# First blocks of x by halves, both differential copies on ScalarE, gate products ahead of weight splits, last router logits ahead of the rank sums

## The chip, the cores and the metric

One Trainium2 chip, one core. The metric is the device time of one launch in microseconds (us); a time given for a kernel is the median of several launches. A launch of the kernel before takes 967.19 us (three runs, 966.83 to 968.14).

Engines: TensorE (PE, matmul and transposes; PEld are its weight loads), VectorE (DVE), ScalarE (ACT), GpSimd (POOL) and SyncE (SP), whose queue issues nearly all DMA here. Each engine works through its own instructions in program order and waits for the others through semaphores.

## What is computed

The reference is one decoder layer on x (512 tokens x 1024, float32), followed by a last RMSNorm:

```python
h = rms_norm(x, g_mix)
fq, fk, fv, f_logit, dq, dk, dv, gate_a, gate_b = split(h @ w_in)
y_a = fox_attention(fq, fk, fv, cumsum(log_sigmoid(f_logit + b)))      # 8 heads of 64, causal
y_b = diff_attention(rope(dq), rope(dk), dv, lam)                       # 4 heads: p1 - lam * p2, causal
y_b = rms_norm(y_b, g_diff_sub) * (1 - lambda_init)
x = x + (sigmoid(gate_a) * (y_a @ w_branch_a) + sigmoid(gate_b) * (y_b @ w_branch_b)) @ w_out
x = x + cross_attention(rms_norm(x, g_cross), rms_norm(mem, g_mem))     # 4 heads, 256 memory tokens
x = x + moe(rms_norm(x, g_ffn))      # top 1 of 4 groups, then top 2 of its 8 SwiGLU experts
return rms_norm(x, g_final)
```

The weights of the 32 experts are 1024 x 512 (gate, up) and 512 x 1024 (down), all float32.

## The kernel before

**Products in two parts.** Every large product is made from operands that are split into a rounded high part and the low rest: `split` (L175 to L177) is a ScalarE copy into the high part (L176) and a VectorE subtraction into the low part (L177). A product then takes three matmuls for each block of 128 of the contraction: high times high, and the two mixed ones (L278 to L280 in the profile). Activations are split into HH and HL (`hh`, `hl` in the profile), weights into `wh` and `wl`.

**Weights of the mixer** come through a stream object `W` in halves of 512 KB: `load` issues the DMA on SP into a raw buffer `wr`, `split` makes `wh` and `wl` of a half, and `W.more()` splits the next half that is due. `W.lazy` says that a unit doesn't call it by itself.

**The first stage** (L318 to L360): x comes in transposed, one block `xT` of 128 x 1024 for each of the four token tiles t. `h_gain` multiplies it by the gain of the norm (VectorE, L326), `h_split` makes hh and hl from it, in two halves of 512 columns each. `nat_unit` (L301) then makes the product with the first 256 columns of the Fox values for tile t: 24 matmuls of 128 x 256 into a bank `fv0p`, and returns its copy out of the bank (L306), which scales by the tile's inverse norm `rT`. The norm itself is taken from the untransposed x: `h_stat(t)` calls `rms_stat` (L251), one ScalarE Square with a sum over 1024 columns, Ln, Exp, and four small VectorE instructions, for each tile. Behind the four units stand the 16 matmuls of the forget logits `pz` (L365, L366), four small ones that spread rT over the partitions (`pR`, L370), and the next unit, `fq0`.

**The attention steps** (L925 to L987): one loop over 16 Fox steps and then 8 Diff steps (two head pairs g, four query tiles b). A Diff step issues in this order: scores (`sd`, L543, with the mask matmuls L673), the softmax (L683 to L685), one unit of other work (a gate unit `w..p` or a branch unit `br`, 24 or 12 matmuls of 128 x 512), the product with the values of the step before, `combine` (VectorE), `W.more()`, the end of the unit's work `ev()`, a second unit, `W.more()` again, the transposes `trans` (`td`, L275), `copy` (L708 to L713) and the second unit's `ev()`. `copy` moves the two transposed banks `td` to `pd` so that the next step's products can read them: the first on VectorE, the second on ScalarE, both recorded at L711. The next step's scores are written to the same four banks, so that they wait for these copies. The end of a gate unit is a VectorE product (L829) and a ScalarE tanh (L830), that of a branch unit a VectorE instruction (L846).

**The routing** (L1315 to L1318): the work behind the output projection follows a table that is written out by hand, one letter for each function. `R` makes the router logits of a token tile (`lg`, 8 matmuls and a ScalarE copy, L1146), `L` transposes them back (`lgt`, L1153, and VectorE L1154), `z` is one step of the ranking of experts (14 small steps for each tile, of which the last writes the mask `Mb`, L1213), `r` sums the mask over the tokens before (`pr`, L1231) and makes the rank `rk` (L1233), `o` makes the one-hot matrix `G` of the first four experts (L1238), `g` gathers tokens with it (`ga`, 4 matmuls for each entry, L1244), and `H` splits the normalised x (`hnh` on ScalarE, L1129; `hnl` on VectorE, L1130).

**The experts** follow: their weights, 4 MB and 2 MB for each expert, stream through a ring of 1 MB pages whose loads are issued on SP (L1269), each as soon as the work on the page's old content is done. `gu` are the gate and up products (L1479).

Order on every engine is that of the code; the framework puts the semaphore waits, and nothing is reordered afterwards.

Of the kernel before, what the change touches and what calls it, by code (L numbers as in the profile page):

```python
# [10 lines left out]
F32 = mybir.dt.float32  # L11
F32R = mybir.dt.float32r
BF = mybir.dt.bfloat16
# [5 lines left out]
P = 128  # L19
# [21 lines left out]
def tile_hybrid_block(  # L41
# [30 lines left out]
    def tiny(shape, name, dt=F32):  # L72
        return work(shape, dt, name, "tiny")
# [11 lines left out]
    def xt(t):  # L85
        return X[t // 2][:, t % 2]
# [20 lines left out]
    def xT(t, k0=0, n=KD):  # L107
        return XT[t // 2][:, t % 2, k0:k0 + n]
# [206 lines left out]
        gemm(o, KD, lambda k: wh[:, k, sl], lambda k: wl[:, k, sl], lambda k: hk(HH, k), lambda k: hk(HL, k))  # L315
        return lambda: evac(j, o)

    def h_split(t, qs=(0, 1)):  # L318

        sl = slice(t * P, (t + 1) * P)  # L320
        for q in qs:
            split(HH[q][:, :, sl], HL[q][:, :, sl], xT(t, 4 * q, 4))

    def h_gain(t, k0=0, n=KD):
        v = xT(t, k0, n)
        V.tensor_tensor(v, v, gm[:, k0:k0 + n, None].to_broadcast([P, n, P]), op=OP.mult)  # L326

    def h_stat(t):
        rms_stat(xt(t), f"nx{t}", out=rT[:, t:t + 1])


    warm = bank("warm", "a")
# [3 lines left out]
    W.lazy = True  # L336
    lg = c1.tile([P, KD, 16], F32R, name="lg")
    h_gain(0, 0, 4)
    h_split(0, (0,))
    W.split(1)  # L340
    h_gain(0, 4, 4)
    h_split(0, (1,))
    W.split(2)
    evs = []
    for t in range(NT):
        evs.append(nat_unit(c_fv[0], t, fv, 0, "fv0", tag="as"[t // 2]))
        if t + 1 < NT:
            h_gain(t + 1)
            h_split(t + 1)
        if t == 1:  # L350
            split(lg[:, :, 0:8], lg[:, :, 8:16], lg_r)
            W.split(3)
        if t == 2:
            h_stat(0)
            h_stat(1)
            evs.pop(0)()
            evs.pop(0)()
            h_stat(2)
            h_stat(3)
    W.lazy = False  # L360


# [296 lines left out]
    class Diff:  # L659
# [47 lines left out]
        def copy(self):  # L707
            self.pt = []  # L708
            for i in range(2):
                r = half([P, S], F32, f"pd{self.g}{self.b}{i}")  # L710
                (V.tensor_copy if i == 0 else A.copy)(r[:, 0:self.n], self.tb[i][:, 0:self.n])  # L711
                self.pt.append(r)

        def av(self):
# [212 lines left out]
    for n, it in enumerate(its):  # L927
        it.scores()
        it.soft()
        while late:  # L930
            late.pop(0)()
        fe = rows() if rows is not None else None
        ev = unit()
        if fe is not None:
            fe()
        fin2 = prev.av() if prev is not None else None
        if n == 1:
            swap_matrix()
        if n == 2:
            rotary_angles()  # L940
        if n == 3:
            rotary_tables()
        if n == 4:
            lam_calc()
        if n == 7:
            dv = page([P, NT, 512], F32, "dv")
        it.combine()
        if fin is not None and isinstance(done, Diff):
            done.scale()
        W.more()  # L950
        if isinstance(it, Diff):
            ev()
            while late:
                late.pop(0)()
            ev = unit()
            W.more()
        it.trans()
        if isinstance(it, Diff):
            it.copy()
            ev()  # L960
        else:
            ev()
            it.copy()
        if n == 5:
            rotary_spread()
        rows = fin
        if isinstance(it, Fox) and it.b == NT - 1 and it.pr < 3:
            Fox(it.pr + 1, 0).prep()
        if n == 15:
            YB["h"] = page([P, 4, S], F32R, "ybh")  # L970
            YB["l"] = page([P, 4, S], F32R, "ybl")
        done, prev, fin = prev, it, fin2
# [342 lines left out]
    for step in """T0 N0 U20 Q0 U21 K0 T1 N1 U30 U22 W Q1 S0 M0 K1 U23 U31 N2 T2 S1 P0 Q2 M1 U32 A0 U33 K2 T3 O0 N3 S2  # L1315
        M2 Q3 P1 X0 K3 F0 A1 S3 M3 P2 R0 O1 L0 P3 F1 z0.0 A2 X1 z0.1 z0.2 z0.3 z0.4
        z0.5 A3 z0.6 z0.7 z0.8 O2 z0.9 z0.10 z0.11 E E E E R1 z0.12 z0.13 H0 X2 F2 L1 r0 O3 o0 z1.0 z1.1 H1 z1.2 z1.3
        F3 z1.4 z1.5 R2 z1.6 z1.7 z1.8 X3 g0.0 z1.9 z1.10 L2 z1.11 z1.12 z1.13 H2 g0.1 z2.0 z2.1 r1 z2.2 R3 o1 z2.3  # L1318
        z2.4 g0.2 z2.5 z2.6 z2.7 L3 z2.8 g0.3 z2.9 z3.0 z2.10 z3.1 g1.0 z2.11 z3.2 z2.12 z3.3 z2.13 H3 g1.1 z3.4 r2
        z3.5 z3.6 o2 z3.7 g1.2 z3.8 z3.9 g1.3 z3.10 z3.11 g2.0 g2.1 z3.12 z3.13 g2.2 g2.3 r3 o3""".split():  # L1320
        f, t = step[0], int(step[1]) if len(step) > 1 else 0
        if f == "U":
            out_unit(t, int(step[2]))
        elif f == "E":
            EX.load(page)
        elif f == "W":
            W.split(2 * c_co + 2)
        elif f == "z":
            route_step(t)
        elif f == "g":  # L1330
            gather0(t, int(step[3]))
        elif f == "M":
            cross_soft(t)
            cross_scale(t)
        else:
            {"N": lambda t: x_stat(t, "nc"), "F": ffn_stat, "r": ranks, "o": lambda t: onehot(0, t), "X": x_trans, "T": cross_trans, "Q": cross_q, "K": cross_qt, "S": cross_scores, "P": cross_ptrans,
             "A": cross_av, "O": cross_out, "H": ffn_split, "R": router,
             "L": router_t}[f](t)
# [510 lines left out]
```

## Time and profile before

| | before |
|---|---|
| median of 3 launches | 967.19 us (966.83 to 968.14) |
| the profiled launch | 968.59 us |
| its span, first to last instruction | 966.8 us |
| mean granted TensorE clock | 0.994 of full speed |
| busy: TensorE, VectorE, ScalarE, GpSimd | 97%, 50%, 33%, 7% |
| read from memory | 243.65 MB |

How to read the rows. A row of the timeline gives the start in us from the span's beginning, the busy time in us, the engine, the line, the operation, output and inputs by their names in the program, the tile's shape, and the count (x2: two such instructions run together). Brackets at the end give the idle time of the engine ahead of the row and what ended it. A row of the view of waits gives the total, the number of times and the longest. A row of the table of windows gives, for a stretch of the span, its length, then the busy time of TensorE, its weight loads, VectorE, ScalarE and GpSimd with the number of instructions in parentheses, then the granted clock, the DMA engines' busy share, and GB/s. The share of busy DMA engines over the span in 40 slices, in tenths, shows where the experts' stream runs (from slice 23 on):

```profile
PE   7999999999999999999999999999999999999995
DMA  8221112221132228335669989999999999999993
```

### The profile page before, as it was taken

What the parts mean: (1) busy time and instruction counts of PE and PEld (TensorE: products, weight loads), DVE (VectorE), ACT (ScalarE), POOL (GpSimd) and SP (SyncE); (2) the same over time, 40 slices, a digit from 0 to 9 for tenths busy, and PEclk for the clock granted to TensorE, in tenths of its full rate; (3) what the DMA queues carried; (4) which work ended last, traced back from release to release, by engine and by line L of the source; (5) the groups of instructions that cost most, each with busy time, mean ns of one, the idle gap of its engine ahead of it and who ended that gap; (6) DMA issues with size and microseconds to landing.
All of it is one profiled execution on the core that took longest, in us unless ns stands there. A gap on an engine that the chain in (4) does not pass through costs nothing. (4 is left out here: it accounts for less than half of the span.)

```text
span 966.8 us, 13460 instructions
## 1 busy us (share of the span) xinstructions
PE 936.9 (97%) x5234; PEld 610.6 (63%) x5235; DVE 484.7 (50%) x1075; ACT 314.3 (33%) x675; POOL 64.5 (7%) x171
## 2 busy tenths in 40 slices
PE   7999999999999999999999999999999999999995
PEld 7787788787887889999743734343633436334332
DVE  6556775857665657655754333443323541243334
ACT  4444444545352445345521211111311112111114
POOL 1840000001111200000100000000000000000000
PEclk9999999999999999999999999999999999999998
DMA  8221112221132228335669989999999999999993
GB/s 320 85 70 66 58 53 66 66 87 44 66 131 87 87 87 283 128 136 233 247 243 411 389 335 420 421 420 422 420 421 421 422 421 420 422 420 421 421 414 119
DMA packets 48290, 246.65 MB, mean 255 GB/s; under 512 B 4832, under 2 KB 12256, under 8 KB 24160
## 3 DMA queue, kind: packets, MB, share of 16 engines
q1 hardware_dynamic: 48080, 245.76, 63.9%
q8 instruction: 42, 0.69, 0.3%
q14 instruction: 24, 0.20, 0.1%
q10 hardware_dynamic: 144, 0.00, 0.0%
HBM read 243.65 MB, written 2.10 MB: 254 GB/s over the span
## 5 line engine op out<-in xcount | busy, mean ns | idle before, releaser
L1479 PE MATMUL gu<-gu,xg 128*64 128x512 f32 x1024 | 223.9, 593 | 1.9 <-DMA gu<-in_w_gu_dram 1.8
L1479 PEld LDWEIGHTS gu<-gu,xg 128*64 128x64 f32 x1024 | 72.7, 137 | 146.4 <-issue 139.1
L1501 PE MATMUL yd<-dn,A 128*64 128x512 f32 x504 | 113.6, 596 | 0.0
L177 DVE TENSOR_TENSOR wl<-wr,wh 128x1024 fp32r<-128x1024 f32 (+1 forms) x66 | 78.1, 1191 | 31.9 <-ACT wh L176 31.2
L1523 DVE TENSOR_TENSOR xr<-cb,xr 128x512 f32<-128x512 f32 x120 | 74.5, 683 | 37.8 <-PE cb L1519 37.7
L1484 DVE SCALAR_TENSOR_TENSOR A<-A,gu 128x256 f32<-128x256 f32 x32 | 13.5, 421 | 157.7 <-ACT A L1483 157.7
L1501 PEld LDWEIGHTS yd<-dn,A 128*64 128x64 f32 x504 | 35.7, 137 | 67.4 <-issue 66.6
L1483 ACT ACTIVATE A<-gu 128x256 f32<-128x256 f32 x32 | 12.3, 383 | 202.2 <-PE gu L1479 202.2
L176 ACT ACTIVATE wh<-wr 128x1024 fp32r<-128x1024 f32 (+1 forms) x66 | 67.0, 1026 | 8.7 <-DVE wr L143 7.7
L1509 DVE SCALAR_TENSOR_TENSOR Y<-yd,ws,Y 128x512 fp32r<-128x512 f32 x32 | 23.9, 751 | 90.4 <-ACT Y L1508 85.6
L1519 PE MATMUL cb<-Y,ohT 128*128 128x512 f32 x240 | 65.0, 410 | 1.6 <-DVE xr L1523 0.5
L1508 ACT ACTIVATE Y<-yd,ws 128x512 fp32r<-128x512 f32 x32 | 21.9, 687 | 119.7 <-PE yd L1501 112.4
L1519 PEld LDWEIGHTS cb<-Y,ohT 128*128 128x128 f32 x240 | 42.9, 188 | 15.4 <-DVE xr L1523 4.3
L278 PE MATMUL wop<-wh,mh 128*128 128x256 f32 x128 | 36.7, 286 | 0.2 <-DVE xr L1023 0.2
L279 PE MATMUL wop<-wl,mh 128*128 128x256 f32 x128 | 36.2, 283 | 0.0
L280 PE MATMUL wop<-wh,ml 128*128 128x256 f32 x128 | 36.2, 283 | 0.0
L1446 PE MATMUL ga<-Gr,hnh 128*128 128x384 f32 x96 | 32.4, 337 | 0.0
L1446 PE MATMUL ga<-Gr,hnl 128*128 128x384 f32 x96 | 32.1, 334 | 0.0
L584 ACT ACTIVATE S<-S,bi 128x128 f32<-128x128 f32 (+3 forms) x32 | 17.8, 556 | 29.7 <-DVE bi L581 29.7
L278 PEld LDWEIGHTS wop<-wh,mh 128*128 128x128 f32 x128 | 24.5, 192 | 0.6 <-DVE xr L1023 0.4
L279 PEld LDWEIGHTS wop<-wl,mh 128*128 128x128 f32 x128 | 24.6, 192 | 0.0
L280 PEld LDWEIGHTS wop<-wh,ml 128*128 128x128 f32 x128 | 24.5, 192 | 0.0
(617 smaller groups left out, 1859.3 us busy)
## 6 DMA issues: line engine op xcount, KB each, us to landing
gu<-in_w_gu_dram SPq DMA_DIRECT2D x128, 1024.0 KB, 19.0
dn<-in_w_dn_dram SPq DMA_DIRECT2D x59, 1024.0 KB, 19.8
wr<-in_w_inp_dram SPq DMA_DIRECT2D x40, 512.0 KB, 3.6
wr<-in_w_out_dram SPq DMA_DIRECT2D x8, 512.0 KB, 5.8
dn<-in_w_dn_dram SPq DMA_DIRECT2D x6, 512.0 KB, 14.4
x<-in_x_dram SPq DMA_DIRECT2D x2, 1024.0 KB, 11.2
wr<-in_w_branch_a_dram SPq DMA_DIRECT2D x4, 512.0 KB, 3.6
wr<-in_w_branch_b_dram SPq DMA_DIRECT2D x4, 512.0 KB, 3.5
```

The costliest lines, as they stand in the source:

```text
L176: A.activation(hi, src, AF.Copy)
L177: V.tensor_tensor(lo, src, hi.bitcast(F32), op=OP.subtract)
L278: PE.matmul(o, lh, rh, start=first, stop=False)
L279: PE.matmul(o, lh, rl, start=False, stop=False)
L280: PE.matmul(o, ll, rh, start=False, stop=last)
L1446: PE.matmul(o, CX[u, t // 2][:, t % 2, kb * P:(kb + 1) * P], CX["G", r][:, t], start=(t == 0 and u == "h"), stop=(t == NT - 1 and u == "l"))
L1479: PE.matmul(gu[64 * f:64 * f + 64, :], xg(2 * i + j), w[:, :, j, 256 * f:256 * f + 256], start=(i + j == 0), stop=(i + j == 4))
L1501: PE.matmul(y[j][64 * a:64 * a + 64, :], hT[a][:, f % 2, f // 2], w(a, f)[:, j, f % 2], start=(f == 0), stop=(f == 3))
L1508: A.activation(yh[rows, j], y[j][rows], AF.Copy, scale=ws)
L1509: V.scalar_tensor_tensor(yl[rows, j], y[j][rows], ws, yh[rows, j].bitcast(F32), op0=OP.mult, op1=OP.subtract)
L1519: PE.matmul(banks[j], oh[:, t * P:(t + 1) * P], y[u][:, j], start=(u == 0), stop=(u == 1))
L1523: V.tensor_tensor(xs, banks[j], xs, op=OP.add)
```

## The change

It edits four places and leaves the arithmetic as it was, apart from the way in which one norm is summed.

1. First stage. The gain product of tiles 1 to 3 is made in two halves of 512 columns, each followed by its high part; the two low parts come behind both. The norms of the four tiles are made by one chain: three Squares on ScalarE and one multiply-and-sum on VectorE for the last tile, then one Ln, one Exp and five VectorE instructions of four columns instead of four chains of one column. The chain stands behind all parts of all tiles. The split of the forget weights `lg` and of the third weight half moves from behind tile 1 to behind tile 2. All four copies out of `fv0p` come behind the matmuls of `pR`; before, two stood ahead.
2. Diff steps. Both copies of `td` to `pd` are on ScalarE.
3. Diff steps. The end of the first unit's work (the gate product, or the branch product) stands ahead of the first `W.more()`.
4. Routing table. `R3` stands ahead of `r1`, the steps of tiles 2 and 3 are interleaved otherwise, and `H3` stands behind the last step of tile 3 instead of ahead of `g1.1`.

```diff
--- before.py
+++ after.py
@@ -315,18 +315,34 @@
         gemm(o, KD, lambda k: wh[:, k, sl], lambda k: wl[:, k, sl], lambda k: hk(HH, k), lambda k: hk(HL, k))
         return lambda: evac(j, o)
 
-    def h_split(t, qs=(0, 1)):
-
+    def h_hi(t, q):
+
+        A.activation(HH[q][:, :, t * P:(t + 1) * P], xT(t, 4 * q, 4), AF.Copy)
+
+    def h_lo(t, q):
         sl = slice(t * P, (t + 1) * P)
-        for q in qs:
-            split(HH[q][:, :, sl], HL[q][:, :, sl], xT(t, 4 * q, 4))
+        V.tensor_tensor(HL[q][:, :, sl], xT(t, 4 * q, 4), HH[q][:, :, sl].bitcast(F32), op=OP.subtract)
 
     def h_gain(t, k0=0, n=KD):
         v = xT(t, k0, n)
         V.tensor_tensor(v, v, gm[:, k0:k0 + n, None].to_broadcast([P, n, P]), op=OP.mult)
 
-    def h_stat(t):
-        rms_stat(xt(t), f"nx{t}", out=rT[:, t:t + 1])
+    def h_stat():
+
+        ss, ln, r0, v, w = (tiny([P, NT], f"nx_{n}") for n in "slrvw")
+        for t in range(NT):
+            junk = work([P, D], BF, f"nx{t}_j")
+            if t < NT - 1:
+                A.activation(junk, xt(t), AF.Square, accum_out=ss[:, t:t + 1])
+            else:
+                V.tensor_tensor_reduce(junk, xt(t), xt(t), 1.0, 0.0, OP.mult, OP.add, ss[:, t:t + 1])
+        A.activation(ln, ss, AF.Ln, scale=1.0 / D, bias=epsd)
+        A.activation(r0, ln, AF.Exp, scale=-0.5)
+        V.tensor_scalar(v, ss, 1.0 / D, 1e-6, op0=OP.mult, op1=OP.add)
+        V.tensor_tensor(w, r0, v, op=OP.mult)
+        V.tensor_tensor(w, w, r0, op=OP.mult)
+        V.tensor_scalar(w, w, -0.5, 1.5, op0=OP.mult, op1=OP.add)
+        V.tensor_tensor(rT, r0, w, op=OP.mult)
 
 
     warm = bank("warm", "a")
@@ -336,27 +352,27 @@
     W.lazy = True
     lg = c1.tile([P, KD, 16], F32R, name="lg")
     h_gain(0, 0, 4)
-    h_split(0, (0,))
+    h_hi(0, 0)
+    h_lo(0, 0)
     W.split(1)
     h_gain(0, 4, 4)
-    h_split(0, (1,))
+    h_hi(0, 1)
+    h_lo(0, 1)
     W.split(2)
     evs = []
     for t in range(NT):
         evs.append(nat_unit(c_fv[0], t, fv, 0, "fv0", tag="as"[t // 2]))
         if t + 1 < NT:
-            h_gain(t + 1)
-            h_split(t + 1)
-        if t == 1:
+            h_gain(t + 1, 0, 4)
+            h_hi(t + 1, 0)
+            h_gain(t + 1, 4, 4)
+            h_hi(t + 1, 1)
+            h_lo(t + 1, 0)
+            h_lo(t + 1, 1)
+        if t == NT - 2:
             split(lg[:, :, 0:8], lg[:, :, 8:16], lg_r)
             W.split(3)
-        if t == 2:
-            h_stat(0)
-            h_stat(1)
-            evs.pop(0)()
-            evs.pop(0)()
-            h_stat(2)
-            h_stat(3)
+            h_stat()
     W.lazy = False
 
 
@@ -708,7 +724,7 @@
             self.pt = []
             for i in range(2):
                 r = half([P, S], F32, f"pd{self.g}{self.b}{i}")
-                (V.tensor_copy if i == 0 else A.copy)(r[:, 0:self.n], self.tb[i][:, 0:self.n])
+                A.copy(r[:, 0:self.n], self.tb[i][:, 0:self.n])
                 self.pt.append(r)
 
         def av(self):
@@ -947,13 +963,13 @@
         it.combine()
         if fin is not None and isinstance(done, Diff):
             done.scale()
-        W.more()
         if isinstance(it, Diff):
             ev()
+            W.more()
             while late:
                 late.pop(0)()
             ev = unit()
-            W.more()
+        W.more()
         it.trans()
         if isinstance(it, Diff):
             it.copy()
@@ -1315,9 +1331,9 @@
     for step in """T0 N0 U20 Q0 U21 K0 T1 N1 U30 U22 W Q1 S0 M0 K1 U23 U31 N2 T2 S1 P0 Q2 M1 U32 A0 U33 K2 T3 O0 N3 S2
         M2 Q3 P1 X0 K3 F0 A1 S3 M3 P2 R0 O1 L0 P3 F1 z0.0 A2 X1 z0.1 z0.2 z0.3 z0.4
         z0.5 A3 z0.6 z0.7 z0.8 O2 z0.9 z0.10 z0.11 E E E E R1 z0.12 z0.13 H0 X2 F2 L1 r0 O3 o0 z1.0 z1.1 H1 z1.2 z1.3
-        F3 z1.4 z1.5 R2 z1.6 z1.7 z1.8 X3 g0.0 z1.9 z1.10 L2 z1.11 z1.12 z1.13 H2 g0.1 z2.0 z2.1 r1 z2.2 R3 o1 z2.3
-        z2.4 g0.2 z2.5 z2.6 z2.7 L3 z2.8 g0.3 z2.9 z3.0 z2.10 z3.1 g1.0 z2.11 z3.2 z2.12 z3.3 z2.13 H3 g1.1 z3.4 r2
-        z3.5 z3.6 o2 z3.7 g1.2 z3.8 z3.9 g1.3 z3.10 z3.11 g2.0 g2.1 z3.12 z3.13 g2.2 g2.3 r3 o3""".split():
+        F3 z1.4 z1.5 R2 z1.6 z1.7 z1.8 X3 g0.0 z1.9 z1.10 L2 z1.11 z1.12 z1.13 H2 g0.1 z2.0 z2.1 R3 z2.2 r1 z2.3 o1
+        z2.4 g0.2 z2.5 z2.6 L3 z2.7 g0.3 z2.8 z3.0 z2.9 z3.1 g1.0 z2.10 z3.2 z2.11 z3.3 z2.12 z3.4 g1.1 z2.13 z3.5
+        z3.6 r2 z3.7 z3.8 o2 g1.2 z3.9 g1.3 z3.10 z3.11 g2.0 g2.1 z3.12 z3.13 H3 g2.2 g2.3 r3 o3""".split():
         f, t = step[0], int(step[1]) if len(step) > 1 else 0
         if f == "U":
             out_unit(t, int(step[2]))
```

Lines behind the first stage have numbers higher by 16 in the changed kernel.

What this does to the order, at the three places that the prediction speaks of. VectorE, the first stage, from tile 2 on, before (`xT` the block and its gain, `hl` the low parts, `wl` the low part of a weight half, `nx_` the norm):

```order
L326 TENSOR_TENSOR xT_84<-xT_84,gm 128x1024
L177 TENSOR_TENSOR hl_115<-xT_84,hh_113 128x4x128
L177 TENSOR_TENSOR hl_116<-xT_84,hh_114 128x4x128
L177 TENSOR_TENSOR lg<-sma,lg 128x8x8
L177 TENSOR_TENSOR wl_217<-wr_94,wh_216 128x1024
L326 TENSOR_TENSOR xT_84<-xT_84,gm 128x1024
L177 TENSOR_TENSOR hl_115<-xT_84,hh_113 128x4x128
L177 TENSOR_TENSOR hl_116<-xT_84,hh_114 128x4x128
L263 TENSOR_SCALAR nx_v<-nx_ss 128x1
```

The same place in the changed kernel:

```order
L328 TENSOR_TENSOR xT_84<-xT_84,gm 128x512 x2
L324 TENSOR_TENSOR hl_115<-xT_84,hh_113 128x4x128
L324 TENSOR_TENSOR hl_116<-xT_84,hh_114 128x4x128
L328 TENSOR_TENSOR xT_84<-xT_84,gm 128x512 x2
L324 TENSOR_TENSOR hl_115<-xT_84,hh_113 128x4x128
L324 TENSOR_TENSOR hl_116<-xT_84,hh_114 128x4x128
L177 TENSOR_TENSOR lg<-sma,lg 128x8x8
L177 TENSOR_TENSOR wl_250<-wr_94,wh_249 128x1024
L338 ISA nx_j,nx_s<-x_76 128x1024
```

The gain products come in halves, and the parts of tile 3 now stand ahead of `lg` and `wl`. The last row is the VectorE sum of squares.

VectorE, the last Diff step of the loop, before (`zn` the normalised output of an earlier step, `g` the branch product):

```order
L736 TENSOR_TENSOR zn_3100<-zo_2805,rq_z 128x512
L177 TENSOR_TENSOR wl_3103<-wr_2853,wh_3102 128x1024
L846 SCALAR_TENSOR_TENSOR g_2779<-g_2779,br_3072 128x512
L711 COPY pd_3132<-td_3122 128x512
L846 SCALAR_TENSOR_TENSOR g_2779<-g_2779,br_3109 128x512
L177 TENSOR_TENSOR wl_3103<-wr_2982,wh_3102 128x1024
```

And in the changed kernel:

```order
L752 TENSOR_TENSOR zn_3071<-zo_2776,rq_z 128x512
L862 SCALAR_TENSOR_TENSOR g_2750<-g_2750,br_3043 128x512
L177 TENSOR_TENSOR wl_3075<-wr_2824,wh_3074 128x1024
L862 SCALAR_TENSOR_TENSOR g_2750<-g_2750,br_3080 128x512
L177 TENSOR_TENSOR wl_3075<-wr_2955,wh_3074 128x1024
```

The branch product has changed places with `wl`, and the copy of `td` is gone from VectorE; it stands on ScalarE, directly ahead of the other.

VectorE, the routing, from the mask of tile 2 on, before (`R` the ranking steps of tile 3):

```order
L1213 TENSOR_TENSOR Mb<-Wh_3886,Wh_3887 128x32
L1130 SCALAR_TENSOR_TENSOR hnl_5075<-xr_3759,nf_z,hnh_5074 128x1024
L1188 ISA R_5119,mm__3888<-L,R_5119 128x32
L1188 ISA mm__3888 128x1
L1233 TENSOR_TENSOR rk<-pr,Mb 128x32
L1191 SCALAR_TENSOR_TENSOR R_5119<-R_5119,mm__3888,down_3872 128x32
L1194 TENSOR_REDUCE R_5119<-R_5119 128x1
L1238 TENSOR_TENSOR G<-rk,slot_f 128x256
```

And in the changed kernel:

```order
L1229 TENSOR_TENSOR Mb<-Wh_3857,Wh_3858 128x32
L1207 SCALAR_TENSOR_TENSOR R_5089<-R_5089,mm__3859,down_3843 128x32
L1210 TENSOR_REDUCE R_5089<-R_5089 128x1
L1249 TENSOR_TENSOR rk<-pr,Mb 128x32
L1213 TENSOR_SCALAR R_5089<-R_5089 128x32
L1254 TENSOR_TENSOR G<-rk,slot_f 128x256
```

`hnl` no longer stands between the mask of tile 2 and its rank `rk` and one-hot matrix `G`; it comes directly behind the mask of tile 3.

## The prediction

> **What bounds the kernel now.** First the page's line of busy times, then the view of waits on TensorE, then two stretches of the table of windows, and SP's waits for the experts' pages.
>
> ```profile
> PE 936.9 (97%) x5234; PEld 610.6 (63%) x5235; DVE 484.7 (50%) x1075; ACT 314.3 (33%) x675; POOL 64.5 (7%) x171
> ...
> PE fv0p L278 <- ACT hh L176: 1.9, 2, 1.0
> PE gu L1479 <- DMA gu<-in_w_gu_dram: 1.8, 1, 1.8
> PE sd L543 <- DVE pd L711: 1.7, 2, 1.2
> ...
> 556.00:561.50 5.50, 5.50 (x27) 2.15 (x28) 2.48 (x4) 1.11 (x2) 0.00 (x0) 1.00 0.28 63
> 582.00:930.00 348.00, 346.19 (x1634) 153.26 (x1632) 124.35 (x235) 58.51 (x113) 0.00 (x0) 1.00 1.01 421
> ...
> SPq L1269 <- PE gu L1479: 84.6, 53, 14.2
> ```
>
> TensorE is busy for 97% of the span, and its waits are short and few, so what the change can win lies in holes of a microsecond. In the experts' part (582 to 930) the DMA engines are full too (share 1.01), and TensorE waits for a page only once, 1.8 us. So a hole that closes ahead of this part could be swallowed by a stream that doesn't move. The first window speaks against that: from 556.0 to 561.5 the DMA engines are busy for 0.28, because the next pages can only be issued when `gu` has read the old ones (SP's largest wait for TensorE in that queue). The full stream begins with TensorE's own progress, and I carry every microsecond won before it 1:1 to the end. All terms below come from the profiled launch: 968.59 us, 1.4 above the median of 967.19 us.
>
> **First stage.**
>
> ```profile
> 3.72 0.69 DVE L326 TENSOR_TENSOR xT<-xT,gm 128x512 f32<-128x512 f32 x1 [2.36 <-DMA gm<-in_small_g_dram]
> 4.44 0.63 ACT L176 ACTIVATE hh<-xT 128x512 fp32r<-128x512 f32 x1 [1.96 <-DVE xT L326]
> ...
> 11.15 1.22 DVE L326 TENSOR_TENSOR xT<-xT,gm 128x1024 f32<-128x1024 f32 x1
> 12.40 1.15 ACT L176 ACTIVATE hh<-xT 128x512 fp32r<-128x512 f32 x2 [2.06 <-DVE xT L326]
> 13.09 0.39 PE L278 MATMUL fv0p<-wh,hh 128*128 128x256 f32 x1 [0.82 <-ACT hh L176]
> 13.81 0.39 PE L280 MATMUL fv0p<-wh,hl 128*128 128x256 f32 x1 [0.22 <-DVE hl L177]
> 16.73 1.04 ACT L176 ACTIVATE wh<-wr 128x1024 fp32r<-128x1024 f32 x1
> 20.89 0.39 PE L278 MATMUL fv0p<-wh,hh 128*128 128x256 f32 x1 [1.05 <-ACT hh L176]
> 21.26 1.04 ACT L256 ACTIVATE nx_j<-x 128x1024 bf16<-128x1024 f32 x1
> 24.35 0.40 PE L365 MATMUL pz<-hh,lg 128*16 128x512 f32 x1
> 28.05 0.83 PE L370 MATMUL pR<-identf,rT 128*128 128x128 f32 x6
> 30.10 0.49 PE L370 MATMUL pR<-identf,rT 128*128 128x128 f32 x2 [1.22 <-DVE rT L249]
> 30.35 0.48 PE L278 MATMUL fq0p<-hh,wh 128*128 128x512 f32 x1
> ```
>
> Tile 1 begins only when a whole gain product (1.22) and a high half (0.63) have run. By halves, the first gain half ends at 11.15 + 0.69 = 11.84, its high half at 12.50, and TensorE starts at 12.56. VectorE does gain b and then `hl` a, both 0.6 to 0.7: ready at 13.22, so that the third matmul starts at 13.28 instead of 13.81. That is 0.53 won. The matmuls of a unit follow each other by 0.12 (24 from 20.89, with one hole of 0.5 at the third, end at 24.35), so tile 3 may begin at 13.28 + 46 x 0.12 + 0.2 = 19.0. VectorE has four halves of 0.65 for each tile, 2.6 us against TensorE's 2.88, and with `lg` and `wl` moved behind tile 3 its low half a is ready at about 18.4. No wait is left at tiles 2 and 3, and `pz` starts at 19.0 + 2.88 = 21.9 instead of 24.35: 2.45 won.
>
> The rest is the norm. `pz` takes 28.05 - 24.35 = 3.70 and ends at 25.6. ScalarE ends its high parts of tile 3 at about 18.3 and `wh` (1.04, now behind them) at 19.4, makes three Squares of 1.04, then Ln and Exp: 23.0. The four small VectorE instructions end by 23.9. The multiply-and-sum over 1024 columns isn't in the trace; VectorE is free for it from 20.6, and rT is in time as long as it ends by 24.1. A single tensor product of that size takes 1.22 (the gain above), two passes would be 2.4: either fits, so it costs nothing. So `pR` finds rT there, the hole of 1.22 at 30.10 goes, eight small matmuls take 0.9, and `fq0` starts at 26.5 instead of 30.35: **3.85 us**. The lower end is 2.4, if rT comes as late as `pR` waits now; the upper is 4.2. The four copies out of `fv0p` moved behind `pR` in the code wait only for rT, and run on ScalarE from 23.9 to 25.6, still ahead of the copy of `pR`. The late `wl` delays the next weight load by some 1.5 us, of halves that are used two units of 5.5 us later.
>
> **Diff steps.**
>
> ```profile
> 230.44 0.39 PE L543 MATMUL sd<-dqk0h 64*128 64x512 f32 x1
> 230.99 0.50 PE L543 MATMUL sd<-dqk0h 64*128 64x512 f32 x1
> 239.02 1.03 PE L275 MATMUL td<-identf,T 128*128 128x128 f32 x8
> 240.09 0.58 ACT L711 COPY pd<-td 128x512 f32<-128x512 f32 x1 [2.87 <-PE td L275]
> 240.73 0.32 PE L543 MATMUL sd<-dqk1h 64*128 64x128 f32 x1 [0.20 <-ACT pd L711]
> 241.49 0.68 DVE L711 COPY pd<-td 128x512 f32<-128x512 f32 x1
> 242.23 0.32 PE L543 MATMUL sd<-dqk1h 64*128 64x128 f32 x1 [1.18 <-DVE pd L711]
> 253.90 0.38 PE L543 MATMUL sd<-dqk1h 64*128 64x256 f32 x1 [0.53 <-DVE pd L711]
> 282.51 0.49 PE L543 MATMUL sd<-dqk1l,dqk1h 64*128 64x512 f32 x1
> 291.27 1.22 DVE L177 TENSOR_TENSOR wl<-wr,wh 128x1024 fp32r<-128x1024 f32 x1
> 292.41 0.68 DVE L846 SCALAR_TENSOR_TENSOR g<-g,br 128x512 f32<-128x512 f32 x1
> 293.14 0.50 PE L278 MATMUL br<-yah,wh 128*128 128x512 f32 x1 [1.58 <-DVE g L846]
> ```
>
> The scores of a step wait for both copies of the step before. ScalarE is idle for 2.87 ahead of its copy at 240.09, while VectorE's comes at 241.49, behind a weight low part. On ScalarE the first copy can start when its bank is full (four of the eight transposes that start at 239.02, so by 239.6) and end at 240.1, and the second runs at its old time. So 240.73 stays, and 242.23 moves to 240.84, one matmul later: 1.39 won. At 253.90 the hole is 0.53 and some 0.25 of refilling; I count 0.75. At 230.99 the matmul follows by 0.55, where this form usually follows by 0.23, so 0.31 goes; the same hole stands at 282.51. Lastly the branch product: at 291.27 `wl` runs first, and TensorE's next unit waits for `g` to free its bank until 293.14. With `g` first it ends at 291.95 and the unit starts at 292.0: 1.1 won. `wl` ends 0.7 later; its half is wanted a unit later. Sum **3.9 us**. What is late next is ScalarE's pair of copies, 0.58 each: had the second to wait for the first in full, 0.5 would come back at each of five steps. So the bounds are 1.4 and 4.4.
>
> **The clock.** The table of windows, cut where the clock changes:
>
> ```profile
> 239.13:242.54 3.41, 2.04 (x21) 1.59 (x19) 3.41 (x6) 0.58 (x1) 0.00 (x0) 1.00 0.13 34
> 242.54:245.95 3.41, 3.41 (x18) 2.91 (x15) 1.80 (x10) 2.20 (x9) 0.00 (x0) 0.50 0.38 125
> ...
> 290.50:293.90 3.40, 1.82 (x12) 1.45 (x11) 3.40 (x6) 1.54 (x2) 0.00 (x0) 1.00 0.09 20
> ```
>
> For exactly 3.41 us behind the stretch with the hole at 242.23 the granted clock was 0.50. Little work of full width lies in it: four transposes at 0.11 more, the masks, and five branch matmuls at 0.2 to 0.35 more, together 1.6 us. If the hole makes the drop, both go. The window at 290.50 was idle for longer and kept 1.00, so that idle time alone doesn't decide it. I take the drop as going, **1.6 us**, in the profiled launch; the timed ones, 1.4 shorter, may not have it at all.
>
> [...]
>
> **Routing.**
>
> ```profile
> 485.24 1.28 DVE L1130 SCALAR_TENSOR_TENSOR hnl<-xr,nf_z,hnh 128x1024 fp32r<-128x1024 f32 x1
> 487.05 0.42 DVE L1238 TENSOR_TENSOR G<-rk,slot_f 128x256 fp32r<-128x256 f32 x1
> 487.52 0.39 PE L1244 MATMUL ga<-G,hnh 128*128 128x256 f32 x1 [0.93 <-DVE G L1238]
> ```
>
> `hnl` of tile 3, 1.28 us, stands between the mask of tile 2 and `G`. Behind the change only two ranking steps (0.2 to 0.3) do, so `G` ends about 1.0 earlier, and `ga` starts at 486.5 instead of 487.52. `hnl` then follows the mask of tile 3, where TensorE gathers tile 2 for 2 us and then sums the ranks; the gather of tile 3 starts behind it. Moving `R3` ahead of `r1` fills an earlier hole of 1.1, but the mask of tile 2 comes from VectorE at its own pace, so I count nothing for it. **0.9 us**; bounds 0 and 2.0 (if the steps of tile 2 run earlier as well).
>
> **Sum.** 3.85 + 3.9 + 0.9 = 8.65; with the clock 10.25. From the profiled launch 968.59 - 10.25 = 958.3; from the median, taken as free of the drop, 967.19 - 8.65 = 958.5. I forecast 958.4.
>
> **Rivals.**
>
> The clock falls anyway, or in another stretch: 968.59 - 8.65 = 959.9. For it: the window at 290.50, which shows that a hole alone doesn't decide. Against: cut into stretches of 3.41 us, the span shows no other drop before TensorE's last matmul. 0.17.
>
> A term stays away: the Diff steps give 1.4 instead of 3.9, because the two copies on ScalarE queue behind each other and the wait turns from VectorE to ScalarE. For it: 240.73 waits for ScalarE already. Against: 2.87 of idle time ahead of that copy. 968.59 - 3.85 - 1.4 - 0.9 = 962.4, or 961 from the median. 0.10.
>
> The change doesn't do what it says, because the expert stream sets the end and doesn't move: nothing is won, 967 to 968.6. For it: share 1.01 up to 930. Against: the gap of 0.28 at 556, which moves with TensorE. 0.04.
>
> Slower: the weight half that now stands behind the gate product.
>
> ```profile
> 223.35 0.48 PE L278 MATMUL w01p<-hh,wh 128*128 128x512 f32 x1
> ...
> 225.76 1.22 DVE L177 TENSOR_TENSOR wl<-wr,wh 128x1024 fp32r<-128x1024 f32 x1 [1.60 <-ACT wh L176]
> ```
>
> On ScalarE `wh` then waits for the tanh, and this for VectorE's product behind `combine`. If the second unit of the step needs that half, it stands still until `wl` is done: as in these rows, 225.76 + 1.22 - 223.35 = 3.6 us in each of four gate steps, 14.5 us, less the 10.25 won: 972.8. It decides as soon as the half is one of the running unit. Against it: in the rows shown that unit ran for 2.4 us before `wl` began, without waiting, so the half belongs to a later unit. 0.03.
>
> **Chances and range.** The forecast as it stands 0.66, the clock 0.17, the Diff steps 0.10, the stream 0.04, slower 0.03. About 0.2%, 1.9 us, is what a measurement of this kernel can tell from no change. Faster by more than that: 0.66 + 0.17 + 0.10 = 0.93; within it 0.04; slower 0.03. The range takes in the lower bounds together (routing 2.0, the steps 4.4: 956.4) and the second rival: 956.2 to 962.2.
>
> **What would show it.** Right: `pz` at 21.9 and `fq0` at 26.5 with no wait of `pR`; no wait of `sd` for a VectorE `pd`; the branch unit near 293.14 within 0.1 us of the transposes' bank; clock 1.00 throughout the Diff steps; `ga` of tile 2 a microsecond earlier; the experts' first full window shifted by the whole sum. Wrong: a wait of `sd` for `pd` of ScalarE, a wait of a unit for `wl`, a drop of the clock in any other stretch behind a hole, or an expert stream that starts at its old time.

## The result and the profile after

The changed kernel takes 957.21 us (four runs, 956.55 to 957.68) against 967.04 us for the kernel before beside it (four runs): a ratio of 0.9898, 95% interval 0.9882 to 0.9913. The forecast was 958.4, range 956.2 to 962.2. The profiled launch took 957.68 us, span 955.9, so 10.91 less than the profiled launch of before; the medians differ by 9.83.

The page's first line and the view of waits on TensorE, of the changed kernel:

```profile
PE 932.1 (98%) x5234; PEld 607.6 (64%) x5235; DVE 482.0 (50%) x1061; ACT 314.3 (33%) x675; POOL 65.3 (7%) x171
...
PE gu L1495 <- DMA gu<-in_w_gu_dram: 2.5, 3, 1.8
...
PE pr L1247 <- DVE Mb L1229: 1.0, 1, 1.0
...
PE br L278 <- DVE g L862: 0.5, 1, 0.5
```

The waits of `sd` for VectorE's `pd`, of `pR` for rT and of `ga` for G are gone from the list; that of `br` for `g` has shrunk from 1.6 to 0.5 (the prediction's sign, within 0.1 us of the transposes' bank, was not reached; the 1.1 us counted for it came, since 1.58 us of idle time became 0.46). The wait of `pr` for the mask (1.1 before) is still there. The wait of `gu` for its pages has grown, from 1.8 in one place to 2.5 in three.

The timeline of the first stage, VectorE and TensorE:

```profile
9.36 0.38 PE L278 MATMUL fv0p<-wh,hh 128*128 128x256 f32 x1 [0.82 <-ACT wh L176]
12.04 0.39 PE L278 MATMUL fv0p<-wh,hh 128*128 128x256 f32 x1 [0.29 <-ACT hh L320]
12.77 0.39 PE L280 MATMUL fv0p<-wh,hl 128*128 128x256 f32 x1 [0.23 <-DVE hl L324]
20.07 1.69 DVE L338 CUSTOM_DVE_ANT_0 nx_j<-x 128x1024 bf16<-128x1024 f32 x1
21.25 0.40 PE L381 MATMUL pz<-hh,lg 128*16 128x512 f32 x1
24.95 1.05 PE L386 MATMUL pR<-identf,rT 128*128 128x128 f32 x8
25.76 0.48 PE L278 MATMUL fq0p<-hh,wh 128*128 128x512 f32 x1
```

The eight matmuls of `pR` run in one piece, and `fq0` starts at 25.76 instead of 30.35. Not all of the 4.59 us is the change's: the matmul at 9.36 waits for the second weight half, which nothing of the change touches, and in before it stood at 9.88. The same row stands at 8.83 to 9.94 in the experiments below, so the first 10 us shift by up to 1.1 us from launch to launch. Without these 0.52 the first stage gives 4.07.

The Diff steps: the first two rows are the scores behind the step whose copies were split between the engines, the third is the branch unit of the last step; the row below them is from the view of waits, for TensorE's weight loads (PEld).

```profile
234.91 0.73 PE L559 MATMUL sd<-dqk1h 64*128 64x128 f32 x2
235.32 0.43 PE L559 MATMUL sd<-dqk1l,dqk1h 64*128 64x128 f32 x2
282.47 0.50 PE L278 MATMUL br<-yah,wh 128*128 128x512 f32 x1 [0.46 <-DVE g L862]
...
PEld sd L559 <- ACT pd L727: 0.3, 1, 0.3
```

The last row is one of the signs of being wrong, a wait of `sd` for a `pd` of ScalarE, and a small one: a weight load waits once for 0.3 us, as it did before.

The table of windows of the changed kernel, first two stretches of 3.41 us in the Diff steps, then the gap ahead of the experts' full stream:

```profile
235.29:238.70 3.41, 3.26 (x22) 2.63 (x23) 2.82 (x10) 1.57 (x9) 0.00 (x0) 1.00 0.39 124
238.70:242.11 3.41, 3.41 (x25) 3.12 (x24) 2.61 (x8) 1.15 (x7) 0.00 (x0) 1.00 0.09 35
544.20:549.70 5.50, 5.50 (x27) 2.19 (x27) 2.45 (x4) 1.06 (x2) 0.00 (x0) 1.00 0.27 74
```

The granted clock stays at 1.00, and the gap in the DMA engines' work (0.27, as 0.28 before) has moved from 556.0 to 544.2, together with TensorE. The branch unit that stood at 293.14 stands at 282.47, so the lead is 10.67 there: 4.59 up to `fq0`, 6.08 since, of which 0.24 came at the scores of the first Diff step (188.06 against 183.16) and 5.84 behind them. In the routing one row carries the gain:

```profile
475.74 0.32 PE L1260 MATMUL ga<-G,hnh 128*128 128x256 f32 x1
```

`ga` of tile 2 stood at 487.52: the lead is now 11.78, 1.1 more. Up to 893 us it stays at 11.8, and at the last matmuls it is 10.9; the rest went in the longer waits for pages.

### The profile page after: what moved, and what is told of

It reads as the page before. It is cut to its first block, busy times and chain, and to the rows that moved or that the text cites. A ratio compares the mean times of both kernels' runs of the same rounds, so it can differ in the third digit from the quotient of the medians.

```text
span 955.9 us, 13447 instructions
## 1 busy us (share of the span) xinstructions
PE 932.1 (98%) x5234; PEld 607.6 (64%) x5235; DVE 482.0 (50%) x1061; ACT 314.3 (33%) x675; POOL 65.3 (7%) x171
```

## The experiments

The kernels come in three groups, each on a chip of its own beside runs of the kernel before (medians 967.25 to 967.41), so the ratios to before are what compares. The changed kernel has 0.9898 (0.9882 to 0.9913).

| kernel | median, us | ratio to before, 95% interval |
|---|---|---|
| old first stage | 961.43 | 0.9939 (0.9926 to 0.9953) |
| old copy | 959.33 | 0.9912 (0.9897 to 0.9927) |
| old order in the step | 958.46 | 0.9909 (0.9892 to 0.9925) |
| both old in the step | 963.01 | 0.9955 (0.9941 to 0.9969) |
| old routing table | 957.84 | 0.9903 (0.9887 to 0.9919) |
| old norm chains | 957.86 | 0.9900 (0.9885 to 0.9916) |
| old copy, hole filled | 957.92 | 0.9902 (0.9887 to 0.9916) |
| g ahead of zn | 956.19 | 0.9883 (0.9867 to 0.9898) |
| r1 later | 958.41 | 0.9906 (0.9892 to 0.9919) |
| Fox copy first too | 963.16 | 0.9958 (0.9946 to 0.9970) |
| 20 matmuls at 480 us | 973.82 | 1.0069 (1.0053 to 1.0085) |
| 20 matmuls at 882 us | 971.45 | 1.0044 (1.0029 to 1.0059) |

Where two ratios differ by less than 0.3% the intervals overlap, and the trace has to say what happened.

### The first stage

The first stage of before, in the changed kernel:

```diff
-            h_gain(t + 1, 0, 4)
-            h_hi(t + 1, 0)
...
-        if t == NT - 2:
+            h_gain(t + 1)
+            h_split(t + 1)
+        if t == 1:
             split(lg[:, :, 0:8], lg[:, :, 8:16], lg_r)
             W.split(3)
-            h_stat()
+        if t == 2:
+            h_stat(0)
...
```

> The changed kernel with the first stage of before (whole gain products, four norm chains); everything else as changed. Theory A (every hole counts 1:1 up to the end): fq0 starts about 4.0 us later than in the changed kernel, the experts' first loads too, and the time is 957.2 + 4.0 = 961.2. Rival B (the experts' stream sets the end by itself and takes up most of a shift): the same 4.0 us later at fq0, but a time under 958.5.

961.43, as theory A has it: `fq0` is 3.35 us later than in the changed kernel though this launch had started 0.53 earlier, so 3.9. At the scores of the first Diff step 0.3 more are lost, which makes 4.2, and this shift stands up to the waits for pages near the end (from 198 to 893 us it changes by less than 0.1). Rival B falls.

The four old norm chains at the new place, the gains by halves:

```diff
-            h_stat()
+            for u in range(NT):
+                h_stat(u)
```

> The changed kernel with the four norms as four chains of one column each (Square, Ln, Exp and four VectorE instructions a tile) at the place of the new chain; the gain products stay by halves. Theory A1 (the halves alone have taken the waits at tiles 1 to 3, and the chain decides only when pR can start): pz starts as in the changed kernel, pR waits for rT by 0.5 to 1.4 us, 957.7 to 958.6. Rival: the place of the chain alone does it (the norms end before pz does): no wait of pR, 957.2.

The timeline of this kernel, TensorE:

```profile
25.99 0.49 PE L373 MATMUL pR<-identf,rT 128*128 128x128 f32 x2 [0.34 <-DVE rT L249]
26.23 0.48 PE L278 MATMUL fq0p<-hh,wh 128*128 128x512 f32 x1
```

`pR` waits again, for 0.34 us, less than the 0.5 of theory A1, and `fq0` starts at 26.23 instead of 25.76 though this launch had started 0.13 earlier (9.23 against 9.36): 0.6 us. The time, 957.86, is 0.65 above the changed kernel's. So the single chain is worth 0.6 of the 4 us; the halves, and the place of everything else behind the parts of tile 3, are the other 3.5.

### The Diff steps

Only the first copy back on VectorE, only the order back, and both:

```diff
-                A.copy(r[:, 0:self.n], self.tb[i][:, 0:self.n])
+                (V.tensor_copy if i == 0 else A.copy)(r[:, 0:self.n], self.tb[i][:, 0:self.n])
```

> The changed kernel with the first copy of td back on VectorE; the gate products stay ahead of the weight splits. Theory A with the clock following the hole: the waits of the scores for VectorE's copies come back (0.31, 1.39, 0.75, 0.31, together 2.8 us) and with the longest of them a stretch of 3.41 us at clock 0.50, 1.6 us: 961.6. Rival C (the drop has another cause than the hole): the waits come back, no stretch of the Diff steps is below 1.00, 960.0. Rival D (the order alone had already taken the waits away): 957.2, no waits.

```diff
+        W.more()
         if isinstance(it, Diff):
             ev()
-            W.more()
             while late:
                 late.pop(0)()
             ev = unit()
-        W.more()
+            W.more()
```

> The changed kernel with the weight split ahead of the first unit's end again; both copies stay on ScalarE. Theory A: the branch unit of the last Diff step waits for g behind wl, 1.1 us later: 958.3. Rival D (with the copies off VectorE the split is no longer in the way): 957.2 to 957.5, no wait above 0.7 us of br for g.

> The changed kernel with both edits of the Diff steps undone. Undone one by one they brought back one hole each (1.4 us of sd for VectorE's copy with the clock's drop; 1.1 us of br for g), while the holes of 0.31, 0.75 and 0.31 came back in neither. Theory E (either edit alone removes these three, since each takes one instruction out of VectorE's way): all five are back, 1.4 + 1.1 + 1.4 = 3.9, with the drop 1.5: 962.6. Rival: the three were gone for the earlier start of the stage: only two are back, 961.2.

The timelines; the old copy (VectorE's weight low parts, then TensorE), then the old order, then both:

```profile
222.03 2.36 DVE L177 TENSOR_TENSOR wl<-wr,wh 128x1024 fp32r<-128x1024 f32 x2 [1.65 <-ACT wh L176]
...
237.19 0.32 PE L559 MATMUL sd<-dqk1h 64*128 64x128 f32 x1 [1.19 <-DVE pd L727]
```

```profile
283.96 0.50 PE L278 MATMUL br<-yah,wh 128*128 128x512 f32 x1 [1.59 <-DVE g L862]
```

```profile
224.44 1.23 DVE L177 TENSOR_TENSOR wl<-wr,wh 128x1024 fp32r<-128x1024 f32 x1 [1.65 <-ACT wh L176]
226.19 0.50 PE L559 MATMUL sd<-dqk0h 64*128 64x512 f32 x1 [0.16 <-DVE pd L727]
...
237.42 0.32 PE L559 MATMUL sd<-dqk1h 64*128 64x128 f32 x1 [1.21 <-DVE pd L727]
249.09 0.38 PE L559 MATMUL sd<-dqk1h 64*128 64x256 f32 x1 [0.55 <-DVE pd L727]
277.71 0.50 PE L559 MATMUL sd<-dqk1h 64*128 64x512 f32 x1 [0.15 <-DVE pd L727]
```

The old copy alone brings back only the longest wait of `sd`, the old order alone only that of `br`. The three smaller waits (226.19, 249.09, 277.71) are listed only when both are undone; of the middle one the old copy alone brings back a third (0.27 us of 0.88 in the starts behind it). Without the copy there is nothing on VectorE for the scores to wait for. With the copy, the new order makes VectorE free for it in time: the weight low part ahead of it ends at 224.4 in the first kernel and at 225.7 in the third, although the first had started 0.4 later, and at 249.09 the branch product no longer stands between the weight half and the copy. So what the two edits save together is more than the sum of what is lost when each is undone alone: 5.9 us against 2.8 and 1.2 by the traces (from 198 us to the branch unit of the last step), 5.5 against 1.35 and 1.05 by the ratios, whose intervals are 1.5 us to either side. Theory E holds (962.6 expected, 963.01 measured), and so does theory A for the old order (958.3, 958.46). The 961.6 for the old copy was 2.3 too high, since the smaller waits stayed away.

### The clock

With the old copy the drop is back. The table of windows, the kernel with the old copy and then the one with the hole filled (the drop starts at 238.60, 0.1 ahead of the second window, hence 0.98 and 0.51):

```profile
235.29:238.70 3.41, 2.03 (x20) 1.63 (x19) 3.13 (x8) 0.59 (x2) 0.00 (x0) 0.98 0.30 103
238.70:242.11 3.41, 3.41 (x10) 2.63 (x9) 2.16 (x9) 1.94 (x9) 0.00 (x0) 0.51 0.15 55
```

```profile
235.29:238.70 3.41, 3.22 (x30) 2.73 (x29) 3.13 (x8) 1.14 (x4) 0.00 (x0) 1.00 0.40 129
238.70:242.11 3.41, 3.41 (x22) 2.98 (x21) 2.13 (x9) 1.64 (x7) 0.00 (x0) 1.00 0.08 30
```

The second kernel is the first one with twelve transposes more in that step, written over the same bank:

```diff
                 t4(self.tb[i], self.p[2 * i], self.b + 1)
+            if self.g == 0 and self.b == NT - 1:
+                for _ in range(3):
+                    t4(self.tb[1], self.p[2], self.b + 1)
```

> The kernel with the old copies, where the hole of 1.4 us at 237.2 was followed by 3.41 us at clock 0.50, with the second td bank of that one step transposed three times more (12 transposes by 0.11): TensorE still waits for VectorE's copy until about 237.2, but works for most of that time. If a lack of any TensorE work makes the drop: no stretch below 1.00 near 239, about 1.5 us less than with the hole, 957.8. If transposes don't count as work, or the drop has another cause: the drop stays, 959.3.

The scores still come only when VectorE's copy is done (236.89 against 237.19, in a launch that had started 0.47 earlier), but TensorE was busy for 3.22 instead of 2.03 of the 3.41 us, the clock stays at 1.00, and by 242 us the lead over the unfilled one has grown from 0.30 to 1.83: the drop costs 1.5 us. So in this place it is the missing work, not the wait, that makes it, and transposes count as work. The time agrees (957.8 expected, 957.92 measured), and so do the mean granted clocks of the timed launches: 0.994 to 0.996 with the hole (five launches), 0.996 and 0.997 with the hole filled (four).

A second place shows the same without being looked for. `r1` and `o1` later in the table, behind two gathers:

```diff
-... H2 g0.1 z2.0 z2.1 R3 z2.2 r1 z2.3 o1
-        z2.4 g0.2 z2.5 z2.6 L3 z2.7 g0.3 z2.8 ...
+... H2 g0.1 z2.0 z2.1 R3 z2.2 z2.3 g0.2
+        L3 g0.3 r1 z2.4 o1 z2.5 z2.6 z2.7 z2.8 ...
```

> The changed kernel with the rank sums of tile 1 and their one-hot matrix later in the table, behind the gathers g0.2 and g0.3. If TensorE still sets the pace in the routing, a wait of up to 1 us goes: 956.2. If VectorE's ranking chain sets it, as I costed the moved logits (nothing), ga of tile 2 starts at the same time after the mask of tile 2 and the time stays: 957.2.

TensorE's two waits there, and the windows that hold them:

```profile
473.05 0.39 PE L1260 MATMUL ga<-G,hnh 128*128 128x256 f32 x1 [0.75 <-DVE G L1254]
475.04 0.18 PE L1247 MATMUL pr<-Mb,ltb 128*128 128x32 bf16 x1 [0.71 <-DVE Mb L1229]
```

```profile
472.28:475.69 3.41, 1.94 (x17) 1.81 (x17) 3.25 (x24) 0.00 (x0) 0.64 (x2) 0.98 0.00 0
475.69:479.10 3.41, 3.41 (x18) 3.41 (x18) 2.47 (x8) 0.00 (x0) 0.43 (x1) 0.52 0.00 0
```

The one hole of 1.0 became two of 0.7, the mask of tile 2 came no earlier (475.04 against 474.68), and the stretch with both holes was followed by a drop. Neither expectation had that: the time went up, in the profiled launch by 1.2 us at the end. The three timed launches with a mean clock of 0.994 or 0.995 took 958.41 to 959.59, the two with 0.996 and 0.997 took 957.77 and 957.45, so most of the loss is the drop. That the mask keeps VectorE's pace agrees with the second.

### The routing table

The old table in the changed kernel (the last of its lines):

```diff
-        z3.6 r2 z3.7 z3.8 o2 g1.2 z3.9 g1.3 z3.10 z3.11 g2.0 g2.1 z3.12 z3.13 H3 g2.2 g2.3 r3 o3
+        z2.4 g0.2 z2.5 z2.6 z2.7 L3 z2.8 g0.3 z2.9 z3.0 z2.10 z3.1 g1.0 z2.11 z3.2 z2.12 z3.3 z2.13 H3 g1.1 z3.4 r2
+        z3.5 z3.6 o2 z3.7 g1.2 z3.8 z3.9 g1.3 z3.10 z3.11 g2.0 g2.1 z3.12 z3.13 g2.2 g2.3 r3 o3
```

> The changed kernel with the routing table of before. Theory A: ga of tile 2 waits for G behind hnl of tile 3 again, 1.2 us in the trace (0.9 by the prediction): 958.1 to 958.4. Rival B (the stream takes it up): under 957.6.

```profile
476.40 0.38 PE L1260 MATMUL ga<-G,hnh 128*128 128x256 f32 x1 [0.93 <-DVE G L1254]
```

The wait for G is back, as long as before (0.93). The time is 957.84, below the expected 958.1 and with an interval that holds the changed kernel's; by the trace `ga` is 0.66 later though the launch had started 0.45 earlier, 1.1 in all. The size rests on the trace alone.

### Does TensorE or the stream set the end

The first matmul of one `gu` product issued 20 times more, in the first call, and in a late one (`calls[0] >= 110`):

```diff
+        if i == 0 and calls[0] >= 1 and calls[0] < 1000:
+            calls[0] = 1000
+            for _ in range(20):
+                PE.matmul(gu[0:64, :], xg(0), w[:, :, 0, 0:256], start=True, stop=True)
```

> The changed kernel with the first matmul of the first gu product issued 20 times more (same result each time), at about 480 us, ahead of the full stream of the experts' weights. It costs TensorE d, by the spacing of gu (eight of them start in 1.9 us) 4 to 9 us, read from the next matmul. Theory A (what happens ahead of the full stream counts 1:1): 957.2 + d. Rival B (the stream's own length sets the end): under 957.2 + d/2.

> The same 20 matmuls, at the 110th call of the same function or the next that begins a product, at about 670 us, inside the full stream. If TensorE sets the end there: 957.2 + d, as in the kernel with the early ones. If the DMA engines do, which are full there while TensorE waits for them at the end: the shift is taken back by the pages that have landed meanwhile, 957.2 to 958.5, and the wait of gu for a page near 921 is shorter by what was taken back.

The timeline of the early one, TensorE:

```profile
480.13 16.95 PE L1499 MATMUL gu<-gu,xg 128*64 128x512 f32 x39
496.50 0.64 PE L1502 MATMUL gu<-gu,xg 128*64 128x512 f32 x1
```

The price d was far above my 4 to 9: each repeat shows as two rows, and these follow each other by 0.43 us, where eight usual ones, which write the two halves of `gu` by turns while the repeats all write the first, took 1.94 us in all. For the 40 rows d is 17.2; the next other instruction, a `ga`, starts at 499.16 instead of 481.94. The shift is still 17.2 at 893 us, and the time rose by 16.6 (973.82 - 957.21): nearly 1:1, and what is lacking is no more than the waits for pages, which are shorter here (1.8) than in the changed kernel's profiled launch (2.5). The other experiments agree: the shift that each of them has at 500 us is the same at 850 us within 0.15 us. The late one landed at 882 us, not 670, since the 110th call comes only at 864 us and the next product begins at 882. Its 40 rows cost as much, and the time rose by 14.2, so that 3.0 were taken back, about what the waits for pages took (2.5 and the refilling behind them), which are gone there. So a shift made ahead of the full stream reaches the end nearly whole, and one made at 882 us reaches it less the waits for pages. A shift made at 670 us wasn't measured.

### Two steps further

The branch and gate products also ahead of `zn`:

```diff
-        if fin is not None and isinstance(done, Diff):
-            done.scale()
         if isinstance(it, Diff):
             ev()
+            if fin is not None and isinstance(done, Diff):
+                done.scale()
             W.more()
```

> The changed kernel with the end of the first unit also ahead of the VectorE product zn of the finished step (0.68 us), which stands ahead of g now. Theory: the two waits of br for g that are left (0.62 at 282.47, 0.28 at 236.76) go and nothing waits for zn: 956.4. Rival: tz waits for zn in the next step, 957.2 or more.

956.19, the fastest of all, ratio 0.9883; its interval overlaps the changed kernel's, so that it beats the kernel before for certain and the changed one probably. In the trace the branch unit behind the last step's transposes starts without a wait, at 282.05, 0.6 us won with the launch's later start; the smaller wait, at 236.76, stays, since the product that it waits for still stands behind the weight half there. So the theory's time came, and half of its reason.

And the copy ahead of the unit's end in the Fox steps too:

```diff
         else:
-            ev()
             it.copy()
+            ev()
```

> The kernel with g ahead of zn (956.2), and in the Fox steps too the copy of the transposed bank ahead of the end of the unit (VectorE's fn and fqk1l, 0.69 each, with a ScalarE copy between them), as the Diff steps have it. Theory: the wait of 0.64 at 98 us (sf for VectorE's pf) and the 0.36 near 183 go: 955.4. Rival: the unit's end, now behind the copy, is late for the next unit's bank: 956.2 or more.

963.16, 7 us worse: the rival. At one of eight such places, VectorE, ScalarE and then TensorE:

```profile
114.27 0.69 DVE L619 COPY pf<-tf 128x512 f32<-128x512 f32 x1 [0.61 <-PE tf L275]
115.19 0.60 ACT L176 ACTIVATE dqk0h<-dq0p 128x512 fp32r<-128x512 f32 x1
115.83 0.69 DVE L177 TENSOR_TENSOR dqk0l<-dq0p,dqk0h 128x512 fp32r<-128x512 f32 x1 [0.86 <-ACT dqk0h L176]
116.58 0.50 PE L663 MATMUL r001s<-dqk0l,swp 128*128 128x512 f32 x1 [0.17 <-DVE dqk0l L177]
```

The copies wait for the transposes, and the parts of the rotated query, which need no transpose, now stand behind them: the high part on ScalarE starts at 115.19, behind the second copy, where the kernel with `g` ahead of `zn` has it at 113.41, and VectorE's low part waits for it. The rotation's matmul and the unit behind it (`dk0p`) lose together 0.7 to 1.2 us at each of the places from 106 to 190 us. The waits at 98 and 183 us did go.

## Why the prediction was right, step by step

**The first stage**, 3.85 forecast: 4.07 in the profiled launch, 3.9 in the trace with the stage undone, both at `fq0`; with the 0.2 to 0.3 at the first Diff step, which come back with the old stage, 4.3 and 4.2, and 4.0 by the ratio. The halves gave the starts that the working has, shifted by the launch's earlier start: tile 1 at 12.04 (12.56 less 0.52), its third matmul at 12.77 (13.28 less 0.52). Both parts of the sum came: `pz` is 2.58 earlier without the 0.52 (2.45 forecast), and from `pz` to `fq0` it takes 4.51 instead of 6.00, 1.49 won (1.4 forecast). What the working didn't part is this 1.4: the single chain is 0.6 of it, and the rest is the norms' new place, where the four old chains would have been late by only 0.34. The multiply-and-sum that the trace of before didn't show took 1.69 us, inside the bounds, and cost nothing.

**The Diff steps**, 3.9 and 1.6 for the clock: 5.84 from the scores of the first step to the branch unit of the last, of which 1.5 is the clock, so 4.3. The second copy does not queue long behind the first, as the rival feared: the pair takes 1.07 us on ScalarE and the scores follow at 234.91 and 235.32. What the working had wrong is whose the three small holes are: it put 0.31, 0.75 and 0.31 down to the copies, and the runs show that the order alone would have closed the first and the last and most of the middle one too. It also had them too small: TensorE's starts behind them give 0.65, 0.85 and 0.65. A part of that was lost again at 236.76, where the branch unit now waits 0.3 for `g`. The longest wait of `sd` is the copies' alone and that of `br` the order's alone, as forecast.

**The clock.** The drop went with the hole, came back with it in two kernels (old copy, both old), and stayed away when the hole was filled; the rival in which it falls anyway is ruled out for the profiled launches. In each of the four traces that have a drop it followed a stretch of 3.41 us with 1.94 to 2.04 us of work, and the clock was then at 0.50 for 3.41 us (before from 242.54, both old from 237.81). That such a stretch is enough for a drop was not shown: the last section has three with less work that no drop followed. For the timed launches the record has the mean granted clock. One drop takes 0.0018 off it (half of 3.41 us in 967), and the half clock behind the last matmul takes 0.0039 in the profiled launch of before (7.5 us) and 0.0031 in that of the changed kernel (6.0 us), so that by this estimate 0.995 or less means at least one drop. All four launches of the changed kernel have 0.996 or 0.997. Of the 29 launches of before beside the experiments 17 have 0.995 or less, and took 967.9 us on average; the other 12 took 966.4, 1.5 less. So the working's premise that the median of before is free of the drop was wrong: more than half of the launches have it, and the 9.83 holds a part of its 1.5.

**The routing**, 0.9: 1.1 in the trace. That the moved logits give nothing was right, since the hole at the mask of tile 2 is still there (1.0) and VectorE sets it.

**1:1 to the end.** Right in kind: the gap ahead of the full stream moved with TensorE, and of 17.2 us put in at 480 us 16.6 came out. Of the 11.8 won by 480 us the profiled launch kept 10.9; 0.7 of the loss are the two more waits for pages. In the experiments whose stream starts 0.5 to 6 us later, one or two such waits remain; the kernel with `g` ahead of `zn`, whose stream starts 0.45 earlier still, has one, so that the earlier start isn't what brings them. Chance of a launch is likely, but wasn't settled.

**The slower rival** did not happen: no unit of the Diff steps waits for a weight half.

Sum: 8.65 without and 10.25 with the clock were forecast, 9.83 is the difference of the medians. That these lie so close is in part luck. By the profiled launches 11.8 was won up to 893 us, 11.3 without the launch's earlier start, 1 us more than forecast (0.45 from the first stage, 0.35 in the Diff steps with the clock, 0.2 in the routing), and about as much was lost again at the pages. The range's upper end, 962.2, is 0.2 below the 962.4 of the second rival that it was to take in; it made no difference here.

## What to carry to other kernels

Before crediting an edit with a hole, ask what else stands ahead of the late instruction on its engine: two edits that each clear the way are worth more together than the two losses when each is undone, and one of them may be enough for most. When a short hole of the busiest engine goes, look at the granted clock in the stretch behind it: the drop here was worth as much as the hole (1.5 us and 1.4). And a copy that has to wait for its input holds up whatever stands behind it: in the Diff steps ScalarE had nothing else to do ahead of it (2.44 us idle), in the Fox steps it held up a product that could have run.

## What the runs showed of the hardware

TensorE's granted clock fell to 0.50 for one stretch of 3.41 us after stretches of that length in which it had worked for 2.04 (before), 2.03 (old copy), 2.01 (both old) and 1.94 us (r1 later, two holes of 0.7). It did not fall in before after 290.50 to 293.90, with 1.82 us of work, nor with the old order behind a hole of 1.59 us at 283.96 (281.60 to 285.00, with 1.81 us of work), nor in the changed kernel behind this stretch with a wait for a page, with 1.57 us of work:

```profile
922.59:926.00 3.41, 1.57 (x10) 0.40 (x8) 0.00 (x0) 0.00 (x0) 0.00 (x0) 1.00 1.00 401
```

So the busy time alone doesn't tell; what does was not found. Filling the hole with transposes, 3.22 us of work in place of 2.03, kept the clock at 1.00.

The copy of 128 x 512 out of a bank of transposes took 0.68 us on VectorE (before, 241.49) and, two of them behind each other, 1.07 us on ScalarE (changed kernel, 234.19).
